# The first stage of a decoder block: where the x blocks are scaled, which engine makes the rotary angles, and the order of the first matmuls

## The chip, the cores and the metric

The kernel runs on one core of a Trainium2 chip. A core has five engines with a queue of instructions each, which run at the same time and wait for one another by semaphores: TensorE (PE in the profile; its weight loads are listed as PEld), VectorE (DVE), ScalarE (ACT), GpSimd (POOL) and SyncE (SP), which here only starts DMA transfers. SBUF is the on-chip memory of 128 partitions, PSUM the eight banks into which TensorE accumulates. The metric is the device time of one execution in microseconds (us), the median of several runs. A profile is one such execution with every instruction's start and end.

## The reference, cut to what matters

One layer of a decoder block on 1024 tokens of width 1024, in float32. What the change touches is the way from the input `x` to the first projection:

```python
ang = positions[..., None] * inv_freq                 # 8 frequencies
cos, sin = cos(ang), sin(ang)                         # rotate the queries and keys
cond = silu(c)
mod = cond @ w_ada + b_ada                            # six rows of 1024
sh_a, sc_a, gt_a, sh_m, sc_m, gt_m = split(mod, 6)
h = rms_norm(x, g_attn_pre) * (1 + sc_a) + sh_a
proj = h @ w_in                                       # 1024 x 2304
...                                                   # two mixers of attention, output projection, MLP
```

`rms_norm` divides each token's row by the root of its mean square and multiplies by a gain.

## The kernel before

**Products in two parts.** TensorE multiplies in a float32 form of fewer bits. So each operand is split: the high part is the value cast to that form, the low part is the value minus the high part. A product is then three matmuls: high x high, low x high, high x low. `hw[:, k, 0]` and `hw[:, k, 1]` are the high and the low part of h, row block k (128 of the 1024 features, all 1024 tokens); `w_hl[i]` holds both parts of a piece of `w_in`.

**The first stage.** `x` comes in as eight blocks of 128 tokens (`load_x`), 512 KB each, then `w_ada` in 16 pieces (`load_ada`, two for each row block k) and `w_in` in pieces (`load_w`), all in SP's queue. For each x block, `x_block(tb)` does:

1. ACT squares the block and sums each row (L652); DVE makes mean plus epsilon of it (`rsqrt_mean`, L477); POOL raises that to the power -1/2 (L480), which gives `rstd`, one number for each token.
2. The block is scaled by it and transposed on TensorE into a PSUM bank in two halves (g = 0, 1). There are two ways. In the first, DVE multiplies the block by `rstd` (L665) and TensorE transposes (L678). In the second (`wide_`), POOL builds a diagonal matrix of `rstd` (`dg`, L661) and TensorE multiplies the block by it (L676), which scales and transposes at once. Blocks 1, 3, 5, 6 and 7 go the second way.
3. ACT or DVE copies each half from PSUM to `xnT` (L686).

`mod_chunk(k)` then makes row block k of h: two reductions on DVE of `w_ada` against the broadcast `cond_b` (`gemv`, L697) give this row block's gain `g_a` and shift `s_a`; ACT applies them and writes the high part (`hi`, L710; for k = 0 in two halves of 512 tokens, L729) and the full value (`full`, L713; for the last k on DVE, L719); DVE subtracts (`lo`, L722). With even k a piece of `w_in` is split, in two halves: the cast on ACT (L557) and the subtraction on DVE (L560).

**The angles.** Position times frequency has to be brought into -pi to pi. This is a chain of 18 small instructions on 64 partitions x 128 elements on DVE (L635 to L641): one product, twice a rounding of two steps, 8 and 4 updates `ang = ang - part * kq`, and a clamp. The sine step `f_sin` on ACT (L746 to L750) loads another function table, makes the sines and cosines, and loads the first table again. Its result goes to DRAM and comes back, spread out, as the tables `cs_t` (L758, L759, L774), which the rotation of queries and keys reads (L826, L831).

**The first unit.** `first_unit` lists the matmuls of the first eight PSUM accumulators (four column blocks c, two halves of tokens) row block by row block, as triples (k, part, accumulator): part 0 is both products with the high part of h (L959, L961), part 1 the one with its low part (L963), and for k = 0 parts 2 and 3 are part 0 taken apart. `AHEAD = 6` row blocks are done for all accumulators before the rest is finished accumulator by accumulator.

**What sets the order.** No instruction is placed by hand. A planner (`Sched`) holds every step with its engine, an estimated duration, its dependences, the buffers it takes and gives, and a priority. It runs a clock for each engine, takes the step that can start first (the priority only breaks ties), and appends its instructions to the queue of that engine. So estimates decide the order in each queue; on the chip the queues then run in that order, and each instruction waits for its real operands. A dependence given to the planner alone (`ready`, `first_hi`, `behind`) thus moves a step in the order without adding a wait for data. `sc.dma`, `LAND` and the bytes per microsecond in `load` are its picture of the DMA.

The value reductions of `mod_chunk(0)` depend, in the planner, on the last block's scaling step, those of chunk 1 on the last eviction but one, and the others on the last four. The sine step depends on the angles and on `full` of chunk 1.

## Time and profile before

| | |
|---|---|
| median of 3 runs | 1112.44 us (1112.32 to 1112.46) |
| profiled execution | 1112.75 us, span of its instructions 1110.9 us |
| TensorE busy | 1091.5 us of the span |
| VectorE busy | 841.4 us |
| ScalarE busy | 648.1 us |
| GpSimd busy | 177.3 us |
| TensorE clock granted | 0.998 of full speed |

Times in the rows of the profile are counted from the start of the span. A row of the order of instructions reads: start, length, engine, line, operation, output <- inputs, shapes, count; in brackets how long the engine had been idle, and what ended that. A group of instructions reads: line, engine, operation, shapes, count | busy us, mean ns | idle us before them. A releaser is inferred from semaphores, and spans on GpSimd are rough. Idle time of an engine that isn't the bottleneck costs nothing by itself.

### The profile page before, as it was taken

What the parts mean: (1) busy time and instruction counts of PE and PEld (TensorE: products, weight loads), DVE (VectorE), ACT (ScalarE), POOL (GpSimd) and SP (SyncE); (2) the same over time, 40 slices, a digit from 0 to 9 for tenths busy, and PEclk for the clock granted to TensorE, in tenths of its full rate; (3) what the DMA queues carried; (4) which work ended last, traced back from release to release, by engine and by line L of the source; (5) the groups of instructions that cost most, each with busy time, mean ns of one, the idle gap of its engine ahead of it and who ended that gap; (6) DMA issues with size and microseconds to landing.
All of it is one profiled execution on the core that took longest, in us unless ns stands there. A gap on an engine that the chain in (4) does not pass through costs nothing.

```text
span 1110.9 us, 15895 instructions
## 1 busy us (share of the span) xinstructions
PE 1091.5 (98%) x5538; PEld 920.9 (83%) x5538; DVE 841.4 (76%) x1480; ACT 648.1 (58%) x1151; POOL 177.3 (16%) x225
## 2 busy tenths in 40 slices
PE   8999999999999999999999999999999999999997
PEld 7888888888988878888888888888888888888885
DVE  8975877888778876789698653898644996537997
ACT  7726666888866766687574234743145632247544
POOL 3004244564622321110000000000000000000003
PEclk9999999999999999999999999999999999999999
DMA  9866767677637526545851378511578013583006
GB/s 362 292 209 211 191 180 230 197 221 224 170 117 211 154 65 227 193 162 226 334 188 39 114 255 332 179 58 44 195 266 313 25 57 114 189 318 137 1 1 152
DMA packets 97432, 198.65 MB, mean 179 GB/s; under 512 B 8328, under 2 KB 31432, under 8 KB 97352
## 3 DMA queue, kind: packets, MB, share of 16 engines
q1 hardware_dynamic: 96632, 195.43, 52.2%
q0 software_dynamic: 576, 2.10, 1.1%
q8 instruction: 44, 0.72, 0.3%
q14 instruction: 36, 0.29, 0.1%
q10 hardware_dynamic: 144, 0.11, 0.0%
HBM read 155.46 MB, written 42.14 MB: 178 GB/s over the span
## 4 chain that ended last, share of the span: by engine, by line
PE 82%; DVE 8%; ACT 3%; DMA 2%; issue 2%; POOL 1%; SPq 0%; POOLq 0%; DVEq 0%; ACTq 0%
PE mlp_ps L2135 18%; PE mlp_ps L2136 18%; PE mlp_ps L2134 18%; PE s_ps L1245 2%; PE y_ps L1678 2%; PE y_ps L1680 2%; PE y_ps L1679 2%; PE pj L959 2%; PE pj L963 2%; PE pj L961 2%; PE o_ps L1379 1%; PE acc L959 1%; PE acc L961 1%; PE acc L963 1%; PE pt_ps L1349 1%
## 5 line engine op out<-in xcount | busy, mean ns | idle before, releaser
L2134 PE MATMUL mlp_ps<-hw 128*128 128x512 f32 x896 | 349.9, 391 | 0.0
L2135 PE MATMUL mlp_ps<-hw 128*128 128x512 f32 x896 | 349.0, 389 | 0.6 <-DVE hw L1899 0.6
L2136 PE MATMUL mlp_ps<-hw 128*128 128x512 f32 x896 | 348.9, 389 | 0.0
L2135 PEld LDWEIGHTS mlp_ps<-hw 128*128 128x128 f32 x896 | 168.3, 188 | 36.1 <-DVE hw L1899 1.0
L2134 PEld LDWEIGHTS mlp_ps<-hw 128*128 128x128 f32 x896 | 168.3, 188 | 35.2 <-issue 0.5
L2136 PEld LDWEIGHTS mlp_ps<-hw 128*128 128x128 f32 x896 | 168.3, 188 | 34.8
L1902 DVE TENSOR_TENSOR hw<-w,hw 128x1024 fp32r<-128x1024 f32 x94 | 111.8, 1223 | 106.7 <-ACT hw L1895 106.5
L1895 ACT CAST hw<-w 128x1024 fp32r<-128x1024 f32 x94 | 95.0, 1047 | 136.8 <-PE mlp_ps L2136 98.7
L2240 POOL TENSOR_TENSOR st<-st,nhalf 128x1 f32<-128x1 f32 x8 | 7.4, 926 | 596.6 <-DVE st L2237 596.5
L1895 ACT CAST hw<-u 128x1024 fp32r<-128x1024 f32 x48 | 48.7, 1052 | 64.6 <-PE mlp_ps L2136 64.6
L1367 DVE TENSOR_TENSOR ph<-pt_ps,ph 128x512 fp32r<-128x512 f32 (+1 forms) x110 | 68.9, 645 | 15.8 <-ACT ph L1363 14.9
L1363 ACT CAST ph<-pt_ps 128x512 fp32r<-128x512 f32 (+1 forms) x110 | 58.8, 555 | 21.7 <-PE pt_ps L1352 17.5
L1275 POOL TENSOR_SCALAR p_sb<-p_sb,den 128x128 f32<-128x128 f32 (+3 forms) x64 | 52.2, 818 | 118.7 <-DVE den L1273 102.5
L1137 POOL TENSOR_TENSOR ada_acc<-ada_acc,wa_st 128x512 f32<-128x512 f32 x42 | 55.8, 1329 | 95.8 <-ACT wa_st L1130 69.7
L1902 DVE TENSOR_TENSOR hw<-u,hw 128x1024 fp32r<-128x1024 f32 x48 | 57.1, 1223 | 16.7 <-ACT hw L1895 16.7
L959 PE MATMUL pj<-hw,w_hl 128*128 128x512 f32 x160 | 68.6, 429 | 0.0
L2192 DVE TENSOR_TENSOR yacc<-yacc,mlp_ps 128x512 f32<-128x512 f32 x96 | 62.6, 688 | 7.1 <-PE mlp_ps L2136 6.9
L963 PE MATMUL pj<-hw,w_hl 128*128 128x512 f32 x160 | 63.2, 395 | 0.0
L961 PE MATMUL pj<-hw,w_hl 128*128 128x512 f32 x160 | 63.0, 394 | 0.0
L1270 ACT ACTIVATE p_sb<-p_sb,mn 128x128 f32<-128x128 f32 (+3 forms) x64 | 49.7, 776 | 21.9 <-DVE mn L1263 20.5
L1678 PE MATMUL y_ps<-hw,oh 128*128 128x512 f32 x120 | 48.6, 405 | 0.9 <-DVE mn L1263 0.9
L1245 PE MATMUL s_ps<-kt,qt 128*128 128x512 f32 (+2 forms) x192 | 48.8, 352 | 0.3 <-DVE mn L1263 0.2
(218 smaller groups left out, 2097.5 us busy)
## 6 DMA issues: line engine op xcount, KB each, us to landing
hw<-s_dram SPq DMA_DIRECT2D x84, 512.0 KB, 4.4
wa_st<-in_w_ada SPq DMA_DIRECT2D x32, 512.0 KB, 5.3
w<-in_w_up SPq DMA_DIRECT2D x32, 512.0 KB, 5.0
w<-in_w_down SPq DMA_DIRECT2D x32, 512.0 KB, 8.9
s_dram<-hw SPq DMA_DIRECT2D x28, 512.0 KB, 4.9
qk_dram<-hl SPq DMA_DIRECT2D x52, 256.0 KB, 3.9
kt<-qk_dram SPq DMA_DIRECT2D x40, 256.0 KB, 6.1
w_st<-in_w_in SPq DMA_DIRECT2D x18, 512.0 KB, 4.6
```

What stands on the lines that cost most here:

```text
L959: T.matmul(ps, wt[:, 0, c0:c0 + P], hw[:, k, 0, t], start=(k == 0), stop=False)
L961: T.matmul(ps, wt[:, 1, c0:c0 + P], hw[:, k, 0, t], start=False, stop=False)
L963: T.matmul(ps, wt[:, 0, c0:c0 + P], hw[:, k, 1, t], start=False, stop=(k == KC - 1))
L1245: T.matmul(s[:, :cw], q_t[u, h, qb // 4][:, qb % 4 * P:qb % 4 * P + P], k_t[u, h, m][:, hl, :cw], start=(hl == 0), stop=(hl == 1))
L1367: V.tensor_tensor(b["ph"][:, 1, :w], b["pt"][:, :w], b["ph"][:, 0, :w].bitcast(F32), ALU.subtract)
L1678: T.matmul(ps[:], oh, wh, start=(k == 4 * i), stop=False)
L1895: A.copy(out[j][0], flat(src[j]))
L1902: V.tensor_tensor(out[j][1], flat(src[j]), out[j][0].bitcast(F32), ALU.subtract)
L2134: T.matmul(ps[m][:], sh, mh, start=starts and k == 0, stop=False, **kw)
L2135: T.matmul(ps[m][:], sh, ml_, start=False, stop=False, **kw)
L2136: T.matmul(ps[m][:], sl, mh, start=False, stop=k == 3, **kw)
L2192: e = op("DVE", t_dv(512), lambda: V.tensor_tensor(y(), y(), ps[m][:], ALU.add), [e, ml.e_y[tb, n]], gives=gives, prio=1)
```

## The change

All of it is in the first stage, and in the planner's picture of it.

- **x blocks.** Only blocks 3 and 5 keep the diagonal. The others are scaled on DVE; the last one in two halves of 512 features, of which the first half's transposes need only the first. The last power therefore goes straight to DVE. Evictions of blocks 0 to 2 are set to DVE, of blocks 4 to 7 to ACT; both evictions of the last block come, in the order, behind the first half of h's row block 0.
- **Angles.** They move to POOL, as 30 instructions: an update becomes a product and an addition. In POOL's queue they stand behind the last block's power. The sine step depends on `full` of chunk 4 instead of chunk 1.
- **Chunks.** All reductions depend, in the planner, on the last block's scaling only, and chunk 0 comes first among ties. `full` of chunk 0 comes behind `hi` of chunk 1.
- **Matmul order.** Row block 0's high products are taken half of the tokens by half, and the low products of row block k come behind the high products of row block k + 1.
- **The broadcast conditioning vector** is copied from PSUM by DVE instead of ACT.
- **The planner's DMA** gets another start, rate and landing time for the first 44 us.

```diff
-LAND = 1.6
+LAND, LAND_FIRST = 1.6, 1.05
...
-            end = self.dma + LAND
+            end = self.dma + (LAND if self.dma > 44 else LAND_FIRST)
...
-        return load(emit, nbytes, [before], takes=[(r, 1) for r in rings], prio=pri(), after=issued)
-
-    sc.dma = 0.5
+        return load(emit, nbytes * 345 / 412, [before], takes=[(r, 1) for r in rings], prio=pri(), after=issued)
+
+    sc.dma = 2.8
...
-            A.copy(cond_b[:, 512 * i:512 * i + 512], cond_ps[i][:])
-    e_cb = op("ACT", 2 * t_ps(512), f_cb, [e], gives=[(r_t, 2)], prio=0)
+            V.tensor_copy(cond_b[:, 512 * i:512 * i + 512], cond_ps[i][:])
+    e_cb = op("DVE", 2 * t_dv(512), f_cb, [e], gives=[(r_t, 2)], prio=3)
...
+    EARLY = 0
+    ON_DVE, ON_ACT = range(0, 6), range(8, 16)
+    WIDE = (3, 5)
...
+    red = p0.tile([64, P], F32, name="red")
+
+    def ts(o, i, c0, c1, f0, f1):
+        return lambda: G.tensor_scalar(o[:], i[:], c0, c1, f0, f1)
+    steps = [ts(ang, posf, inv_f[0:64], 1.0, ALU.mult, ALU.mult)]
...
+        steps += [ts(kq, ang, inv, ROUND, ALU.mult, ALU.add), ts(kq, kq, -ROUND, 0.0, ALU.add, ALU.add)]
         for part in parts:
-            steps += [lambda part=part: V.scalar_tensor_tensor(ang[:], kq[:], -part, ang[:], ALU.mult, ALU.add)]
...
+            steps += [ts(red, kq, -part, 1.0, ALU.mult, ALU.mult),
+                      lambda: G.tensor_tensor(ang[:], ang[:], red[:], ALU.add)]
+    steps += [ts(ang, ang, 3.1415925, -3.1415925, ALU.min, ALU.max)]
+    dg_last = Later()
     e = e_pos
-    for f in steps:
-        e = op("DVE", 0.22, f, [e, e_c], prio=1)
+    for i, f in enumerate(steps):
+        e = op("POOL", 0.45, f, [e, e_c] + [dg_last] * (i >= EARLY), prio=8)
...
-        wide_ = tb % 2 or tb == TB - 2
+        wide_ = tb in WIDE
...
-        else:
+        elif tb < TB - 1:
             e = op("DVE", t_d2(D) + AP_DV,
                    lambda: V.tensor_scalar(x_t[tb][:], x_t[tb][:], rstd[:, tb:tb + 1], None, ALU.mult), [e], prio=2)
+        else:
+            for i in range(2):
+                def f_sc(c=slice(512 * i, 512 * i + 512)):
+                    V.tensor_scalar(x_t[tb][:, c], x_t[tb][:, c], rstd[:, tb:tb + 1], None, ALU.mult)
+                e = es[i] = op("DVE", 0.42, f_sc, [e], prio=-1)
         e_scaled[0] = e
+        if tb == TB - 1:
+            dg_last.ev = e
...
-            e_xn.append(op(("ACT", "DVE"), (t_ps(512), t_dv(512)), (ev(A.copy), ev(V.tensor_copy)), [d] + [first_hi] * (tb == TB - 1 and g),
-                           gives=[(r_b, 1)], prio=2))
+            on = slice(1, 2) if 2 * tb + g in ON_DVE else slice(0, 1) if 2 * tb + g in ON_ACT else slice(0, 2)
+            e_xn.append(op(("ACT", "DVE")[on], (t_ps(512), t_dv(512))[on], (ev(A.copy), ev(V.tensor_copy))[on],
+                           [d] + [first_hi] * (tb == TB - 1), gives=[(r_b, 1)], prio=2))
...
-        ready = [e_scaled[0]] if k < 1 else e_xn[14:15] if k < 2 else e_xn[-4:]
+        ready = [e_scaled[0]]
...
-                gives=[(r_wa, 1)], prio=2)
+                gives=[(r_wa, 1)], prio=-1 if k < 1 else 2)
...
-            e = e_full[k] = op("ACT", t_sb(S) + 2 * AP_COST, full, e_hh[k], prio=0)
+            e = e_full[k] = op("ACT", t_sb(S) + 2 * AP_COST, full, e_hh[k] + [next_hi] * (not k), prio=0)
...
-    e_sin = op("ACT", 3.4, f_sin, [e_ang, e_full[1]], prio=0)
+    e_sin = op("ACT", 3.4, f_sin, [e_ang, e_full[4]], prio=0)
...
-        order = [(0, part, (c, half)) for part in (2, 3) for half in range(2) for c in (1, 0, 3, 2)]
-        order += [(k, part, a) for k in range(AHEAD) for part in range(not k, 2) for a in every]
+        order = [(0, part, (c, half)) for half in range(2) for part in (2, 3) for c in (1, 0, 3, 2)]
+        for k in range(1, AHEAD):
+            order += [(k - part, part, a) for part in range(2) for a in every]
+        order += [(AHEAD - 1, 1, a) for a in every]
```

More of the change, by code (lines that the diff above doesn't have):

```diff
@@ L633, in hybrid_block @@
     cs = p0.tile([64, 3, P], F32, name="cs")
-    steps = [lambda: V.tensor_scalar(ang[:], posf[:], inv_f[0:64], None, ALU.mult)]
+    red = p0.tile([64, P], F32, name="red")
+    def ts(o, i, c0, c1, f0, f1):
+        return lambda: G.tensor_scalar(o[:], i[:], c0, c1, f0, f1)
+    steps = [ts(ang, posf, inv_f[0:64], 1.0, ALU.mult, ALU.mult)]
     for inv, parts in ((1.0 / (TWO_PI * 4096), COARSE), (1.0 / TWO_PI, FINE)):
-        steps += [lambda inv=inv: V.tensor_scalar(kq[:], ang[:], inv, ROUND, ALU.mult, ALU.add),
-                  lambda: V.tensor_scalar(kq[:], kq[:], -ROUND, None, ALU.add)]
+        steps += [ts(kq, ang, inv, ROUND, ALU.mult, ALU.add), ts(kq, kq, -ROUND, 0.0, ALU.add, ALU.add)]
         for part in parts:
-            steps += [lambda part=part: V.scalar_tensor_tensor(ang[:], kq[:], -part, ang[:], ALU.mult, ALU.add)]
-    steps += [lambda: V.tensor_scalar(ang[:], ang[:], 3.1415925, -3.1415925, ALU.min, ALU.max)]
+            steps += [ts(red, kq, -part, 1.0, ALU.mult, ALU.mult),
+                      lambda: G.tensor_tensor(ang[:], ang[:], red[:], ALU.add)]
+    steps += [ts(ang, ang, 3.1415925, -3.1415925, ALU.min, ALU.max)]
+    dg_last = Later()
     e = e_pos
-    for f in steps:
-        e = op("DVE", 0.22, f, [e, e_c], prio=1)
+    for i, f in enumerate(steps):
+        e = op("POOL", 0.45, f, [e, e_c] + [dg_last] * (i >= EARLY), prio=8)
     e_ang = e
@@ L655, in x_block @@
         e = rsqrt_mean(rstd[:, tb:tb + 1], ssq[:, tb:tb + 1], D, 1, e, prio=0)
-        wide_ = tb % 2 or tb == TB - 2
+        wide_ = tb in WIDE
+        es = [None, None]
         box = {}
@@ L660, in f_dg @@
                 box["d"] = p0.tile([P, P], F32, name="dg", tag="dg", bufs=2)
-                G.tensor_scalar(box["d"][:], ident, rstd[:, tb:tb + 1], 1.0, ALU.mult, ALU.mult)
-            e = op("POOL", 0.39, f_dg, [e], takes=[(r_dg, 1)], prio=0)
-        else:
+                if tb < TB - 1:
+                    G.tensor_scalar(box["d"][:], ident, rstd[:, tb:tb + 1], 1.0, ALU.mult, ALU.mult)
+                else:
+                    V.tensor_scalar(box["d"][:], ident, rstd[:, tb:tb + 1], None, ALU.mult)
+            e = op("POOL" if tb < TB - 1 else "DVE", 0.39 if tb < TB - 1 else 0.25, f_dg, [e], takes=[(r_dg, 1)], prio=0)
+        elif tb < TB - 1:
             e = op("DVE", t_d2(D) + AP_DV,
                    lambda: V.tensor_scalar(x_t[tb][:], x_t[tb][:], rstd[:, tb:tb + 1], None, ALU.mult), [e], prio=2)
+        else:
+            for i in range(2):
+                def f_sc(c=slice(512 * i, 512 * i + 512)):
+                    V.tensor_scalar(x_t[tb][:, c], x_t[tb][:, c], rstd[:, tb:tb + 1], None, ALU.mult)
+                e = es[i] = op("DVE", 0.42, f_sc, [e], prio=-1)
         e_scaled[0] = e
+        if tb == TB - 1:
+            dg_last.ev = e
         r_x_ = r_stg if tb in IN_STG else r_wa
@@ L678, in tr @@
                         T.transpose(box[g][:, k], xk, ident)
-            d = pe_op("xt", 0.9 if wide_ else 0.46, tr, [e], takes=[(r_b, 1)],
+            d = pe_op("xt", 0.9 if wide_ else 0.46, tr, [es[g] or e], takes=[(r_b, 1)],
                       gives=([(r_x_, 1)] + [(r_dg, 1)] * wide_) if g else [])
@@ L724, in mod_chunk @@
             e_hh[k] = [op("ACT", t_sb(S) + 2 * AP_COST, hi, [e1, e2] + e_xn[k // 4::2], prio=0)] * 2
+            if k == 1:
+                next_hi.ev = e_hh[k][0]
         else:
```

3 lines of the change are left out of this document (2 added, 1 removed).

## The prediction

> **What bounds the kernel now.** I read the page's totals first, then a table of stages, then the chain of waits, then the order of instructions on each engine in the first 45 us.
>
> ```profile
> span 1110.9 us, 15895 instructions
> PE 1091.5 (98%) x5538; PEld 920.9 (83%) x5538; DVE 841.4 (76%) x1480; ACT 648.1 (58%) x1151; POOL 177.3 (16%) x225
> ```
>
> TensorE (PE) is busy for 98% of the span. The table of stages (stretch, its length, busy time of each engine with its count, granted clock, DMA share, GB/s) says where the rest is:
>
> ```profile
> 0.00:24.00 24.00, 19.26 (x135) 17.52 (x136) 19.73 (x68) 16.84 (x31) 10.86 (x17) 1.00 0.92 354
> 24.00:60.00 36.00, 36.00 (x160) 29.65 (x160) 32.51 (x44) 26.46 (x31) 0.00 (x0) 1.00 0.75 273
> 600.00:700.00 100.00, 100.00 (x440) 82.47 (x440) 53.75 (x58) 41.00 (x56) 0.00 (x0) 1.00 0.62 222
> ```
>
> From 24 us on PE hardly stops. So a microsecond by which PE's projection starts earlier is one off the end, if PE is then fed without a gap, and a new gap in the projection is one on the end. Before 24 us PE does only warm-up and transposes. The chain of waits there (start, length, what):
>
> ```profile
> 17.35 2.80 POOL rstd L480
> 20.23 0.89 POOL dg L661
> 21.16 1.17 PE pxt L676 x8
> 22.41 0.58 ACT xnT L686
> 23.00 0.72 ACT hw L729
> 23.76 2.11 PE acc L959 x8
> 33.15 1.81 PE acc L963 x8
> ```
>
> The projection starts at 23.76, and what it waits for is the last x block: the power on GpSimd (POOL), its diagonal, the scaling transposes, an eviction, and h's first half row. The power is far longer than its kind. In the order of instructions (start, length, engine, line):
>
> ```profile
> 8.42 0.55 POOL L480 TENSOR_TENSOR rstd<-rs_t,nhalf 128x1 f32<-128x1 f32 x1 [0.93 <-DVE rs_t L477]
> 16.74 0.37 POOL L661 TENSOR_SCALAR dg<-head,rstd 128x128 f32<-128x128 f32 x1
> 15.99 0.19 ACT L652 ACTIVATION_READ_ACCUMULATOR xnT<-x_sb 128x1 f32 x1
> 17.12 0.14 DVE L477 TENSOR_SCALAR rs_t<-ssq 128x1 f32<-128x1 f32 x1
> 17.18 1.33 DVE L697 CUSTOM_DVE_ANT_0 wa<-wa,cond_b,bb 128x1024 f32<-128x1024 f32 x1
> 17.35 2.79 POOL L480 TENSOR_TENSOR rstd<-rs_t,nhalf 128x1 f32<-128x1 f32 x1 [0.23 <-DVE rs_t L477]
> 18.45 1.28 DVE L697 CUSTOM_DVE_ANT_0 wa<-wa,cond_b,bb 128x1024 f32<-128x1024 f32 x1
> 20.23 0.88 POOL L661 TENSOR_SCALAR dg<-head,rstd 128x128 f32<-128x128 f32 x1
> 20.26 0.70 DVE L560 TENSOR_TENSOR w_hl<-w_st,w_hl 128x512 fp32r<-128x512 f32 x1 [0.52 <-ACT w_hl L557]
> ```
>
> The power takes 0.55 at 8.42 and 2.79 at 17.35. In between, VectorE (DVE) runs the two reductions of w_ada chunk 0 (L697) until 18.45 + 1.28 = 19.73, and the power ends 0.41 after that. The diagonal takes 0.37 alone and 0.88 beside a subtraction that ends at 20.96; it ends 0.15 later. So a POOL instruction that reads SBUF stands still while DVE runs one with two SBUF inputs. This observation carries the forecast, in both directions.
>
> **The change, part by part: the gain.** The last block loses its diagonal (0.88) and its slow power: the reductions of chunk 0 now come behind the block's scaling. Its transposes become plain ones. The statistics step (L477) starts at 17.12, though its square's sum is there at 16.18 (15.99 + 0.19): DVE's queue held two evictions and the angles' last step ahead of it. Both kinds leave DVE, so I start from 16.2. The prices of the rest:
>
> ```profile
> L665 DVE TENSOR_SCALAR x_sb<-x_sb,rstd 128x1024 f32<-128x1024 f32 x3 | 2.2, 745 | 0.2 <-POOL rstd L480 0.2
> L729 ACT ACTIVATE hw<-xnT,s_a,g_a 128x512 fp32r<-128x512 f32 x2 | 1.5, 809 | 0.0
> L619 ACT COPY cond_b<-cond_ps 128x512 f32<-128x512 f32 x2 | 1.1, 577 | 0.0
> L640 DVE SCALAR_TENSOR_TENSOR ang<-kq,ang 64x128 f32<-64x128 f32 x12 | 3.4, 285 | 0.1
> ```
>
> Statistics 0.15, power 0.55, two half scalings 0.8 (one whole is 0.745, each half pays its start again: estimate), two reductions 2.55, handovers 0.1: 16.2 + 4.15 = 20.35. Then h's first half row, 0.8, whose eviction (blocks 0 to 3) is long done: PE starts at 21.2 instead of 23.76, 2.55 earlier. The half scalings and the transposes of the last block lie beside the reductions; h's second half is needed 8 matmuls (1.8 us) later, and two evictions and the activation (about 1.9 us on ScalarE, ACT) take as long: 0 to 0.3 lost. Chunk 1 is the next bound. It must be done when 16 matmuls of row block 0 are, at 21.2 + 16 x 0.2265 = 24.8 (0.2265 is the pitch of the chain's matmuls, 1.81 for 8 at 33.15). DVE reaches it at 21.07, as its first row below shows for before, then 2 x 1.27 and ACT's 1.24: 24.9. I take **2.4 us** for the whole gain (2.55 less 0.15), with 1.4 and 2.6 as ends: the lower one if a half of w's split stands ahead of chunk 1 (0.7) and POOL slows DVE by 0.3.
>
> The conditioning copies (0.58 each) change from ACT to DVE and three more blocks are scaled on DVE (3 x 0.745) where three diagonals fall away; the 12 steps of 0.285 and six others leave DVE. All this lies before 16.2 us, where x comes in at the DMA's pace: +-0.3, in the ends. That h's low products come one row block later moves 8 matmuls; it removes none.
>
> **The change, part by part: the loss.** 30 angle steps (one, twice two, 12 updates that now need two instructions each, and the clamp: 18 with one input, 12 with two) go to POOL behind the last power. A 64 x 128 step on POOL isn't in the trace. Its nearest rows are the 0.37 above and the power's 0.55: about 0.42, so 30 steps alone take some 12.5 us, from 16.9 to 29.4. They won't be alone. From 21 to 45 us DVE did this (groups: count, busy us, mean ns), without a pause:
>
> ```profile
> L697 DVE CUSTOM_DVE_ANT_0 wa<-wa,cond_b,bb 128x1024 f32<-128x1024 f32 x11 | 14.2, 1314 | 0.1
> L722 DVE TENSOR_TENSOR hw<-xnT,hw 128x1024 fp32r<-128x1024 f32 x5 | 6.1, 1223 | 0.4 <-ACT xnT L713 0.4
> L560 DVE TENSOR_TENSOR w_hl<-w_st,w_hl 128x512 fp32r<-128x512 f32 x5 | 3.4, 688 | 0.0
> 30.00:40.00 10.00, 10.00 (x45) 8.19 (x45) 10.00 (x16) 9.94 (x15) 0.00 (x0) 1.00 1.01 398
> 21.09 1.35 DVE L697 CUSTOM_DVE_ANT_0 wa<-wa,cond_b,bb 128x1024 f32<-128x1024 f32 x1
> ```
>
> 21 instructions in 24 us, 1.14 each, all with two SBUF inputs. What such a neighbour does to POOL shows again later:
>
> ```profile
> 487.25 1.63 POOL L1725 TENSOR_TENSOR st<-rs_t,nhalf 128x1 f32<-128x1 f32 x1 [5.07 <-DVE rs_t L1723]
> 487.25 1.23 DVE L1902 TENSOR_TENSOR hw<-h,hw 128x1024 fp32r<-128x1024 f32 x1
> 488.39 1.22 DVE L2067 TENSOR_TENSOR sum_T<-w,sum_T 128x1024 f32<-128x1024 f32 x1
> 202.90 2.26 DVE L560 TENSOR_TENSOR w_hl<-w_st,w_hl 128x1024 fp32r<-128x1024 f32 x1
> ```
>
> At 487 the power gets in between two DVE instructions, at 17.35 it had to let two go by, and at 202.90 DVE waited for POOL. So POOL gets one step through for each DVE instruction at best (a step's first 0.2 us passes before it asks, and by then DVE has started the next), and one for two at worst. I take one for one, the nearer to most rows.
>
> [...]
>
> Who waits for the angles? The sine step on ACT, which now stands behind the full row of chunk 4, and behind it in ACT's queue h's chunks 5 to 7 (and the table writes on SP's queue, and what SP has behind those):
>
> ```profile
> 28.50 1.28 ACT L746 ACT_TABLE_LOAD   x1
> 32.26 0.31 ACT L750 ACTIVATE ang<-kq 64x128 f32<-64x128 f32 x1
> 61.99 0.69 DVE L826 TENSOR_TENSOR hl<-acc,cs_t 64x512 f32<-64x512 f32 x1 [2.91 <-PE acc L963]
> 40.21 1.24 ACT L713 ACTIVATE xnT<-xnT,s_a,g_a 128x1024 f32<-128x1024 f32 x1
> 44.25 1.25 ACT L710 ACTIVATE hw<-xnT,s_a,g_a 128x1024 fp32r<-128x1024 f32 x1 [2.29 <-DVE s_a L697]
> 51.13 0.39 PE L959 MATMUL acc<-hw,w_hl 128*128 128x512 f32 x1
> ```
>
> The sine step takes 32.57 - 28.50 = 4.1 with its two table loads. Chunk 4's full row ran at 40.21; ACT no longer makes the sine detour before it, but DVE sets its pace, so ACT reaches the sine step at about 41. By then DVE has ended 5 such instructions before 21 and (41 - 21) / 1.14 = 17 after: 22 angle steps done, 8 left. DVE still has work of its own that doesn't need ACT (chunks 5, 6, half of 7), so 8 x 1.0 more: angles at 49, sine at 53.1, h's chunk 5 at 54.3. PE wants chunk 5 (first used at 51.13 now) 2.4 earlier, and 8 matmuls (1.8) earlier again since a low product has moved behind it: 46.9. PE waits **7.4 us**. Ends: 3.9 us if a step comes through every 0.95 us (16.9 + 30 x 0.95 = 45.4, and 5.3 for sine and chunk 5); 12 if POOL gets in once for two DVE instructions: DVE's own work, some 28 instructions, ends at 21 + 23 x 1.14 = 47 with 14 steps done, and 16 x 0.42 more make it 53.7.
>
> Once fed, PE isn't held again: chunks 6 and 7 each have 5.4 us of its matmuls ahead of them against ACT's 2.5. The rotation tables come 11 us later than the sine (writes and loads on SP's queue: estimate), at 64, and the first accumulator, which the rotation takes up at 61.99 now, would then be done near 67.
>
> **The sum.** The profiled execution took 1112.75 us (span 1110.9 and 1.85 around it), 0.3 over the median of the runs. 1112.75 - 2.4 + 7.4 = 1117.75; as a median **1117.4 us**.
>
> **Rivals.** (1) **The angles keep up.** If a step comes through every (41.6 - 16.9) / 30 = 0.82 us or faster, they are done when ACT gets to the sine or just after, chunk 5 is ready at 41.6 + 5.3 = 46.9, and the gain stands: 1112.4 - 2.4 = 1110.0. For it: 12.5 us of work have 24.7 us of room, and DVE may pause for landings. Against it: the 17.35 and 20.23 rows, and DVE's 10.00 of 10. This is the case of the other sign, and 0.82 us a step is where it begins. (2) **Gain and stall cancel.** With 0.85 to 0.95 us a step PE waits 0.8 to 3.9 us: 1110.9 to 1113.9, say 1112.4. (3) **The start doesn't move as far**, since the last x block lands as before and ACT's evictions stand ahead of its squares: gain 1.4, so 1111.0 in rival 1 and 1118.4 in my case.
>
> **How the numbers follow.** Late angles 0.47 (its own range 1113.9 to 1122), keeping up 0.38, cancelling 0.15. Faster and slower count from 0.2% (2.2 us), about what a measurement can tell. Faster: 0.34, nearly all of rival 1 (the rest, 0.04, with the small gain of 3, is within). Slower: 0.48, the late angles and a little of the cancelling case. Within: 0.18. Rival 3 is a smaller gain inside either case, with 0.15 of each. Range 1109.7 to 1121.5, from nearly the full gain of rival 1 to just under POOL's worst rate, as cases of both signs hold most of the chance.
>
> **What would show it.** Right: the projection's first matmul near 21.2; the last power at 0.55; angle steps on POOL of 1 us and more from 21 us on, the last near 49; ACT idle ahead of the sine's table load, released by POOL; PE idle ahead of row block 5, near 47. Wrong: angle steps mostly under 0.8 us, or the sine load right behind chunk 4's full row; then rival 1 holds. The start of the projection at 22.5 or later would break the gain.

## The result, and the profile after

The changed kernel takes 1118.86 us (median of 6 runs, 1117.86 to 1120.33) against 1112.45 us before (6 runs, 1111.78 to 1112.69): a ratio of 1.0059, with a 95% interval of 1.0049 to 1.0069. It is slower by 6.4 us. The forecast was 1117.4, in a range of 1109.7 to 1121.5. The profiled execution of the changed kernel took 1117.86 us, 5.1 more than the profiled one of before.

The page's totals of the changed kernel say that TensorE (PE) does the same work in a longer span, and GpSimd (POOL) 25 us more of its own (177.3 before):

```profile
span 1116.1 us, 15864 instructions
PE 1091.7 (98%) x5514; PEld 918.8 (82%) x5514; DVE 841.8 (75%) x1463; ACT 649.4 (58%) x1154; POOL 202.3 (18%) x252
```

The table of stages of the changed kernel (stretch, length, busy time of PE, its weight loads, DVE, ACT and POOL with their counts, granted clock, DMA share, GB/s) shows where. Before, PE was busy for 36.00 of the 36 us of the first row:

```profile
24.00:60.00 36.00, 30.18 (x123) 23.67 (x122) 31.44 (x42) 24.60 (x28) 24.14 (x23) 0.95 0.61 227
600.00:700.00 100.00, 100.00 (x440) 82.42 (x440) 53.69 (x55) 40.98 (x55) 0.00 (x0) 1.00 0.56 202
```

In the 36 us of the first projection PE now lacks 5.8 us, VectorE (DVE) and ScalarE (ACT) are less busy too, and the mean granted clock is 0.95 instead of 1.00. The long MLP stage, in the second row, is as before. So the loss lies between 24 and 60 us. In the order of instructions on POOL there (start, length, engine, line; L641 and L647 are the angle steps), a selection:

```profile
16.15 0.99 POOL L480 TENSOR_TENSOR rstd<-rs_t,nhalf 128x1 f32<-128x1 f32 x1 [0.33 <-DVE rs_t L477]
17.13 0.36 POOL L641 TENSOR_SCALAR ang<-posf,head 64x128 f32<-64x128 f32 x1
...
21.08 0.62 POOL L641 TENSOR_SCALAR red<-kq 64x128 f32<-64x128 f32 x1
21.78 1.34 POOL L647 TENSOR_TENSOR ang<-ang,red 64x128 f32<-64x128 f32 x1
...
48.87 1.15 POOL L641 TENSOR_SCALAR ang<-ang 64x128 f32<-64x128 f32 x1
```

The first step takes 0.36 and the second 0.34, the later ones 0.62 to 1.49, and the last ends at 48.87 + 1.15 = 50.02: 30 steps in 32.9 us, 1.10 each. What stands behind them on ACT, and then on PE (L769 to L773 is the sine step, L731 h's high part, L982 and L984 the first unit's matmuls; the bracket is the idle time before, and what ended it), in the same view of the changed kernel:

```profile
40.84 1.24 ACT L734 ACTIVATE xnT<-xnT,s_a,g_a 128x1024 f32<-128x1024 f32 x1
42.61 1.28 ACT L769 ACT_TABLE_LOAD   x1
50.05 0.31 ACT L769 ACTIVATE cs<-ang 64x128 f32<-64x128 f32 x1 [6.15 <-POOL ang L641]
51.20 1.28 ACT L773 ACT_TABLE_LOAD   x1
52.72 1.23 ACT L731 ACTIVATE hw<-xnT,s_a,g_a 128x1024 fp32r<-128x1024 f32 x1
...
21.59 1.20 PE L982 MATMUL acc<-hw,w_hl 128*128 128x512 f32 x4 [1.44 <-ACT hw L752]
26.39 0.50 PE L984 MATMUL acc<-hw,w_hl 128*128 128x512 f32 x1 [0.35 <-DVE w_hl L560]
53.99 0.80 PE L982 MATMUL acc<-hw,w_hl 128*128 128x512 f32 x1 [4.95 <-ACT hw L731]
```

PE starts the projection at 21.59 instead of 23.76, 2.17 us earlier. At 42.61 ACT comes to the sine, loads the table, and stands for 6.15 us until POOL has the angles. Chunk 5 of h, behind the sine in ACT's queue, is ready at 53.95; PE had run out of other matmuls and starts row block 5 at 53.99, after an idle time of 4.95. Then comes something that the forecast doesn't have. The same stretch of the changed kernel in windows of 2 us (stretch, length, PE's busy time and count, granted clock, DMA share, GB/s):

```profile
52.00:54.00 2.00, 0.01 (x1) 0.87 0.21 49
54.00:56.00 2.00, 2.00 (x5) 0.50 0.22 50
56.00:58.00 2.00, 2.00 (x9) 0.77 0.90 286
58.00:60.00 2.00, 2.00 (x10) 1.00 0.93 256
```

After the gap the granted clock is 0.50 for some 3 us. The first eight matmuls take 3.29 us (53.99 to 57.28) where eight take 1.81: 1.5 us more are lost. The rotation takes up the first accumulator at 68.14 instead of 61.99, and the MLP starts at 494.49 instead of 489.25.

### The profile page after: what moved, and what is told of

Read it like the earlier page. It is cut to its first block, busy times and chain, and to the rows that moved or that the text cites. A ratio compares the mean times of both kernels' runs of the same rounds, so it can differ in the third digit from the quotient of the medians.

```text
span 1116.1 us, 15864 instructions
## 1 busy us (share of the span) xinstructions
PE 1091.7 (98%) x5514; PEld 918.8 (82%) x5514; DVE 841.8 (75%) x1463; ACT 649.4 (58%) x1154; POOL 202.3 (18%) x252
## 4 chain that ended last, share of the span: by engine, by line
PE 85%; DVE 7%; POOL 3%; ACT 2%; issue 2%; DMA 0%; POOLq 0%; DVEq 0%; SPq 0%; ACTq 0%
PE mlp_ps L2160 17%; PE mlp_ps L2159 17%; PE mlp_ps L2161 17%; PE pj L982 3%; PE pj L986 3%; PE pj L984 3%; PE s_ps L1270 3%; PE y_ps L1703 2%; PE y_ps L1705 2%; PE y_ps L1704 2%; PE s_ps L1324 2%; PE o_ps L1404 2%; POOL ang L647 1%; PE o_ps L1415 1%; PE pt_ps L1374 1%
## 5 line engine op out<-in xcount | busy, mean ns | idle before, releaser
L1300 POOL TENSOR_SCALAR p_sb<-p_sb,den 128x128 f32<-128x128 f32 (+3 forms) x64 | 50.8, 797 | 104.8 <-DVE den L1298 83.7
L982 PE MATMUL pj<-hw,w_hl 128*128 128x512 f32 x160 | 68.1, 426 | 0.0
L984 PE MATMUL pj<-hw,w_hl 128*128 128x512 f32 x160 | 63.0, 393 | 0.0
L1270 PE MATMUL s_ps<-kt,qt 128*128 128x512 f32 (+2 forms) x192 | 48.9, 353 | 0.9 <-DMA qt<-qk_dram 0.4
```

The lines of the kernel that those rows point to most:

```text
L982: T.matmul(ps, wt[:, 0, c0:c0 + P], hw[:, k, 0, t], start=(k == 0), stop=False)
L984: T.matmul(ps, wt[:, 1, c0:c0 + P], hw[:, k, 0, t], start=False, stop=False)
L1270: T.matmul(s[:, :cw], q_t[u, h, qb // 4][:, qb % 4 * P:qb % 4 * P + P], k_t[u, h, m][:, hl, :cw], start=(hl == 0), stop=(hl == 1))
```

## The experiments

Late angles (theory L, the prediction's) blame the queue: the sine waits on ACT, and chunk 5 behind it. The rivals at first were P, that GpSimd's angle steps slow DVE beside them wherever the sine stands, and O, that the loss comes from the new matmul order or the evictions. All runs together, in us; "start" is PE's first projection matmul, "rotation" the first instruction of DVE that takes up an accumulator (L826 before, L849 after the change), "MLP" PE's first MLP matmul, all from the profiled execution:

| kernel | median (lowest to highest) | ratio to before, 95% interval | start | rotation | MLP | profiled |
|---|---|---|---|---|---|---|
| before | 1112.45 (1111.78 to 1112.69) | | 23.76 | 61.99 | 489.25 | 1112.75 |
| changed | 1118.86 (1117.86 to 1120.33) | 1.0059, 1.0049 to 1.0069 | 21.59 | 68.14 | 494.49 | 1117.86 |
| 1 coarse updates out | 1112.06 (1111.56 to 1113.04) | 0.9997, 0.9987 to 1.0006 | 21.89 | 61.02 | 488.29 | 1111.64 |
| 2 sine one chunk later | 1113.97 (1112.62 to 1115.25) | 1.0013, 1.0003 to 1.0022 | 21.41 | 61.82 | 490.53 | 1113.89 |
| 3 angles from the start | 1116.19 (1114.53 to 1117.10) | 1.0032, 1.0020 to 1.0044 | 22.88 | 63.00 | 491.21 | 1115.70 |
| 4 angles on VectorE | 1117.17 (1116.81 to 1119.13) | 1.0047, 1.0031 to 1.0064 | 22.82 | 64.73 | 493.36 | 1116.81 |
| 5 angles alone | 1117.27 (1116.88 to 1119.25) | 1.0045, 1.0030 to 1.0060 | 22.22 | 67.41 | 493.93 | 1117.38 |
| 6 matmul order of before | 1117.83 (1115.09 to 1118.95) | 1.0043, 1.0028 to 1.0058 | 21.95 | 66.24 | 495.56 | 1118.95 |
| 7 gap filled | 1118.60 (1117.50 to 1119.22) | 1.0053, 1.0038 to 1.0068 | 22.39 | 67.60 | 494.10 | 1117.50 |
| 8 planner's price | 1116.25 (1115.00 to 1117.33) | 1.0032, 1.0020 to 1.0045 | 21.35 | 69.32 | 492.65 | 1116.09 |
| 9 angles shared | 1113.65 (1113.35 to 1115.03) | 1.0014, 1.0005 to 1.0023 | 21.23 | 64.44 | 490.19 | 1113.59 |
| 10 shared, in one piece | 1111.84 (1111.03 to 1114.37) | 0.9997, 0.9988 to 1.0006 | 21.46 | 61.42 | 488.38 | 1111.78 |

The kernel before ran beside each group of runs, with medians of 1112.28 (runs 1 to 4), 1112.47 (5 to 8), 1112.31 (9) and 1112.83 (10); the ratios are to those. From the MLP's start on all of them take 623.4 us, to 0.1 (run 3 1.1 more), so what differs has come in by then. The start itself varies by some 0.6 us either way among the runs whose first 20 us are alike (the changed kernel and 1, 2, 7, 8, 9 and 10).

### 1: the coarse updates left out

```diff
-                      lambda: G.tensor_tensor(ang[:], ang[:], red[:], ALU.add)]
+                      lambda: G.tensor_tensor(ang[:], ang[:], red[:], ALU.add)] if parts is FINE else [lambda: None] * 2
```

> The changed kernel with its 16 coarse update instructions of the angles left out (the angles are then not reduced; nothing else is left out, and every queue keeps its order). Theory L (late angles block the scalar engine's queue, and so row block 5 of h): 14 steps of about 1.05 us from 17.1 end near 32, the sine step runs at 42.6 without a wait, h's row block 5 is ready near 48 where TensorE wants it at 48.9; TensorE's gap of 5.1 us and its slow 3 us after it go: 6.6 us less than the changed kernel's 1118.9, so 1112.3, down to 1111.3 if TensorE's two small waits in row blocks 1 and 3 go too. [...] Rival O (the new matmul order or the evictions made the loss): 1118 to 1119.

Measured: 1112.06. In the order of instructions of this kernel, POOL's last angle step, ACT's table load and the first rotation:

```profile
30.20 1.15 POOL L641 TENSOR_SCALAR ang<-ang 64x128 f32<-64x128 f32 x1
41.94 1.28 ACT L769 ACT_TABLE_LOAD   x1
61.02 0.69 DVE L849 TENSOR_TENSOR hl<-acc,cs_t 64x512 f32<-64x512 f32 x1 [2.90 <-PE acc L986]
```

With 14 steps instead of 30 the angles are there at 31.35, 10 us before ACT wants them, PE has no gap, and 6.8 us of the changed kernel's 1118.86 are gone. So the 16 steps cost 6.8 us; this run alone doesn't tell their lateness from what they do to DVE beside them (run 2 does). What is left of the change is worth 0.2 us by the medians (1112.06 against 1112.28), no difference that can be measured (the interval reaches from 1.4 us faster to 0.7 slower), although PE starts 1.87 us earlier than before. 0.6 of that goes ahead of row block 1, where PE waits for the split of w on DVE (L560: PE's matmuls at 25.68 and 26.53 lie 0.85 apart instead of 0.2265), another 0.3 in smaller pieces; at the rotation 0.97 is left.

### 2: the sine one chunk later

```diff
-    e_sin = op("ACT", 3.4, f_sin, [e_ang, e_full[4]], prio=0)
+    e_sin = op("ACT", 3.4, f_sin, [e_ang, e_full[5]], prio=0)
```

> The changed kernel with the sine step behind the full row of chunk 5 instead of chunk 4; all angle steps stay where they are, TensorE's queue is the same. Theory L: row block 5 is ready near 45, the angles still end near 50, the sine at 52.8, row block 6 near 54 where TensorE wants it at 56; the tables land near 61.3, in time for the first accumulator near 61.5. So 1112.3 (1118.9 - 6.6), with all of VectorE's and GpSimd's delays still there. Rival P: the steps are unchanged, so 1118 to 1119. Rival O: the same, 1118 to 1119.

Measured: 1113.97, where L said 1112.3. The sine on ACT, and PE much later, in the order of instructions of this kernel:

```profile
49.85 0.31 ACT L769 ACTIVATE cs<-ang 64x128 f32<-64x128 f32 x1 [2.45 <-POOL ang L641]
...
372.49 0.50 PE L1404 MATMUL o_ps<-ph,v_hl 128*128 128x256 f32 x2 [2.01 <-DVE ot L1444]
```

and the clock behind that last row, in this kernel's windows of 2 us:

```profile
372.00:374.00 2.00, 1.51 (x6) 0.74 0.54 144
374.00:376.00 2.00, 2.00 (x10) 0.50 0.79 228
```

In the first stage L is right: chunk 5 stands ahead of the sine, PE has no gap there, although the angles come no earlier (49.81) and ACT waits for them as well, and the rotation starts at 61.82. One moved instruction takes 4.9 us off the changed kernel, with all 30 steps in place; the 1118 to 1119 of P and O falls. P isn't nothing, though: from PE's start to the rotation run 2 needs 40.41 us (61.82 - 21.41) and run 1, with 16 steps fewer, 39.13, so up to 1.3 of run 1's 6.8 us are what GpSimd does to DVE. Of the 1.7 us that are missing 1.5 lie between the rotation and the MLP (428.7 us, 427.3 before), in the attention stage: PE waits 2.01 us at 372 and then runs at half clock again. With the change the planner also writes another order for that stage. The kernel before has no such wait; the changed one, whose order on PE is the same as in run 2, has it with 1.42 us (377.58) and without a fall of the clock. What makes it 2.01 here is not settled. Four of the ten executions take 1112.62 to 1113.06, near L's number, the others up to 1115.25.

### 3 and 4: the angles elsewhere

Run 3 lets the steps begin as soon as the positions are there; run 4 puts them back on VectorE in their form of before and leaves the rest of the change.

```diff
-    EARLY = 0
+    EARLY = 30
```

```diff
-        e = op("POOL", 0.45, f, [e, e_c] + [dg_last] * (i >= EARLY), prio=8)
+        e = op("DVE", 0.22, f, [e, e_c], prio=1)
```

> The changed kernel with the angle steps free to start as soon as the positions are there, so that they stand between the powers of the x blocks in GpSimd's queue instead of behind the last one. Theory L: while VectorE mostly evicts PSUM, a step takes 0.35 to 0.5 us; a power waits up to 0.5 us for the step ahead of it, so the projection starts 0.3 to 0.8 us later than 21.6; the angles end near 30, the sine no longer waits: 1110.5 to 1112.5. Rival P: the same number of steps beside the same VectorE work, 1116 or more. Rival O: 1118 to 1119.

> The changed kernel with the angles on VectorE as before (18 instructions), all else changed, the sine still behind chunk 4. Theory L: the gain of the change without its loss. 18 x 0.28 = 5 us go back into VectorE's queue ahead of 18 us; where they fit between x blocks the projection starts near 22 and the time is 1110.5, where they don't it starts near 23.5 and the time is 1112. Rival O: 1116 or more, as the angles aren't the cause.

Measured: 1116.19 and 1117.17. L missed both; by the numbers alone P's "1116 or more" is met in run 3 and O's in run 4. The traces show another reason than theirs. The gap ahead of row block 5 is gone in both, as L says; but the angles now stand in the way of the x blocks. Run 3, PE and POOL in the order of instructions:

```profile
35.84 1.15 POOL L641 TENSOR_SCALAR ang<-ang 64x128 f32<-64x128 f32 x1
...
22.88 1.19 PE L982 MATMUL acc<-hw,w_hl 128*128 128x512 f32 x4 [1.04 <-ACT hw L752]
28.67 0.50 PE L984 MATMUL acc<-hw,w_hl 128*128 128x512 f32 x1 [0.89 <-DVE w_hl L560]
```

Run 4, DVE and PE in the same view:

```profile
21.88 0.74 DVE L673 TENSOR_SCALAR x_sb<-x_sb,rstd 128x1024 f32<-128x1024 f32 x1
...
14.65 0.66 PE L693 MATMUL pxt<-head,x_sb 128*128 128x128 f32 x4 [2.50 <-DVE rs_t L477]
22.82 1.18 PE L978 MATMUL acc<-hw,w_hl 128*128 128x512 f32 x4 [0.55 <-ACT hw L748]
24.07 1.94 PE L693 MATMUL pxt<-head,x_sb 128*128 128x128 f32 x16
27.52 1.20 PE L978 MATMUL acc<-hw,w_hl 128*128 128x512 f32 x4 [0.81 <-ACT hw L748]
```

In run 3 the steps stand between the powers, the last power starts at 17.34 instead of 16.15, PE starts at 22.88 and then waits 0.89 for w's split. Up to 17 us its steps take 0.29 to 0.65; from 19.68 on, beside DVE's reductions and subtractions, 0.62 to 1.54. In run 4 one whole block is scaled only at 21.88, behind both reductions of chunk 0; PE starts at 22.82, but 16 transposes then stand between its first matmuls, and h's second half comes at 27.52. Both also have the wait near 374 us (1.95 and 1.74), with a granted clock of 0.50 in a window of 2 us behind it. In the profiled executions run 3 is 1.0 us later than before at the rotation, another 0.95 at the MLP and another 1.0 at the end, the last for no reason that a run shows; run 4 is 2.7 later at the rotation and another 1.4 at the MLP. So with the angles among the x blocks, on either engine, PE's early start is lost in part, and the waits behind it take more than what is left.

### 5: the angles alone

The kernel before, with the steps on GpSimd and the sine behind chunk 4's full row, as in the change; everything else as before.

```diff
-    steps = [lambda: V.tensor_scalar(ang[:], posf[:], inv_f[0:64], None, ALU.mult)]
+    steps = [ts(ang, posf, inv_f[0:64], 1.0, ALU.mult, ALU.mult)]
...
-        e = op("DVE", 0.22, f, [e, e_c], prio=1)
+        e = op("POOL", 0.45, f, [e, e_c] + [dg_last], prio=8)
...
-    e_sin = op("ACT", 3.4, f_sin, [e_ang, e_full[1]], prio=0)
+    e_sin = op("ACT", 3.4, f_sin, [e_ang, e_full[4]], prio=0)
```

> The kernel before with one part of the change: the 30 angle steps on GpSimd behind the last block's work and the sine step behind chunk 4's full row; scaling, conditioning copies and matmul order as before. Theory L (late angles hold ScalarE's queue): the steps start near 21 us, after the last diagonal, and take 1.10 us each as in the changed kernel, so they end at 54; the sine needs 2.7 more, chunk 5 another 1.2: ready at 58. TensorE wants it near 51.5, waits 6.5 us and then runs at half clock for about 3 us (1.5 lost): 1112.4 + 8 to 8.5 = 1120 to 1121, worse than the whole change. Rival O (the loss comes from the new matmul order or the scaling, not from the angles): 1114 or less.

Measured: 1117.27; L's 1120 to 1121 was 3 us too much, rival O falls. In the order of instructions of this kernel:

```profile
19.51 0.37 POOL L638 TENSOR_SCALAR ang<-posf,head 64x128 f32<-64x128 f32 x1
49.45 0.29 POOL L638 TENSOR_SCALAR ang<-ang 64x128 f32<-64x128 f32 x1
...
22.22 2.12 PE L966 MATMUL acc<-hw,w_hl 128*128 128x512 f32 x8 [0.55 <-ACT hw L736]
54.23 0.80 PE L966 MATMUL acc<-hw,w_hl 128*128 128x512 f32 x1 [4.09 <-ACT hw L717]
```

This one part gives 4.8 of the 6.4 us, with the same gap ahead of row block 5. What the expectation didn't have: without the angles on DVE the kernel before starts at 22.22 already. That is 1.54 of the 2.17 us by which the whole change moves the start. Its statistics step comes at 16.68 instead of 17.12, and its power gets in after one reduction, where before it had to let two go by:

```profile
16.91 1.58 POOL L480 TENSOR_TENSOR rstd<-rs_t,nhalf 128x1 f32<-128x1 f32 x1 [0.29 <-DVE rs_t L477]
```

That is 1.58 instead of 2.79, and most of the 1.54. The halves, the reductions' places and the evictions together add some 0.6, no more than the start scatters by. The steps began at 19.51, earlier than I had them, took 30.2 us, 1.01 each, and the gap was 4.1 instead of 6.5.

### 6: the matmul order of before

```diff
-        order = [(0, part, (c, half)) for half in range(2) for part in (2, 3) for c in (1, 0, 3, 2)]
-        for k in range(1, AHEAD):
-            order += [(k - part, part, a) for part in range(2) for a in every]
-        order += [(AHEAD - 1, 1, a) for a in every]
+        order = [(0, part, (c, half)) for part in (2, 3) for half in range(2) for c in (1, 0, 3, 2)]
+        order += [(k, part, a) for k in range(AHEAD) for part in range(not k, 2) for a in every]
```

> The changed kernel with the matmul order of before in the first unit (each chunk's low-part products directly behind its high-part products, not one row block later). Theory L: chunk 5 is ready at 54 us whatever TensorE does before, and 8 matmuls (1.8 us) that now stand behind that point stand ahead of it again, inside the gap: the gap falls from 5.1 to 3.3 us, the first accumulator comes 1.8 us earlier (66.3 instead of 68.1), 1116.0 to 1117.0. A stall for a low part before chunk 5 (up to 3 us) would be inside the gap too and cost nothing. Rival O (the new order saves more than 1.8 us of waits earlier): 1118.9 or more.

Measured: 1117.83, first rotation at 66.24 (L: 66.3). The rotation came out as expected by luck, for it got there by another way. PE in the order of instructions of this kernel, and then its windows:

```profile
23.62 1.74 PE L982 MATMUL acc<-hw,w_hl 128*128 128x512 f32 x4 [0.48 <-ACT hw L752]
30.06 3.13 PE L986 MATMUL acc<-hw,w_hl 128*128 128x512 f32 x8 [1.82 <-DVE hw L743]
```

```profile
24.00:26.00 2.00, 2.00 (x6) 0.51 1.03 414
32.00:34.00 2.00, 2.00 (x6) 0.50 1.02 408
```

With the old order PE waits early: 0.48 us for h's second half, soon after the 1.44 ahead of its start, and 1.82 us for a low part of h (L743), both times with half clock after it. So it is late by itself, and there is no gap left ahead of row block 5. The new matmul order (row block 0 half by half, the low parts one row block later) spares these waits. But chunk 5 comes at 54.3 all the same, and all that PE saves ahead of it ends in the gap. The whole isn't told apart from the changed kernel: at 1115.09 to 1118.95 the four runs scatter too far, and this profiled one has the attention wait with 2.04 us on top.

### 7: the gap filled

```diff
+            def fillers():
+                for i in range(22):
+                    T.matmul(accs[every[i % 8]][:], zt[:], hw[:, 4, 0, 0:512], start=False, stop=False)
+            if k == 5 and part == 0 and a == every[0]:
+                dense(0.0, fillers, [])
```

> The changed kernel with 22 more matmuls (128 x 512, a weight tile of zeros, so they add nothing to the accumulators) ahead of row block 5 on TensorE: 22 x 0.2265 = 4.98 us of work where TensorE waited 5.1 us. Nothing else is changed. Theory C (the half clock after the gap comes from TensorE standing idle): the clock stays at 1.00, the 1.5 us behind the gap fall away, first accumulator at 66.6 instead of 68.1, 1116.4 to 1117.4. Rival (the clock falls for another reason, such as all engines starting at once behind the wait): the clock falls as before, 1117.9 to 1119.

Measured: 1118.60, profiled 1117.50. The 22 matmuls in the order of instructions, and PE's windows around them:

```profile
49.69 5.31 PE L1006 MATMUL acc<-hw,zt 128*128 128x512 f32 x22
```

```profile
48.00:52.00 4.00, 4.00 (x19) 1.00 0.00 0
52.00:56.00 4.00, 4.00 (x18) 1.00 0.17 40
56.00:60.00 4.00, 4.00 (x19) 1.00 0.79 238
```

The clock stays at 1.00 throughout, and from PE's start to the first rotation it takes 45.21 us instead of 46.55: 1.34 less, with 22 matmuls more. So the half clock comes from PE standing idle (theory C), not from the restart. On the whole time this doesn't show; 1118.60 lies in the rival's range, and only the trace speaks for C. The start lay 0.8 us later in this execution (22.39), and single runs scatter by more than the 1.3 us.

### 8: the planner told the price

```diff
-        e = op("POOL", 0.45, f, [e, e_c] + [dg_last] * (i >= EARLY), prio=8)
+        e = op("POOL", 1.10, f, [e, e_c] + [dg_last] * (i >= EARLY), prio=8)
```

> The changed kernel with one number of the planner altered: an angle step on GpSimd is entered at 1.10 us, as the trace of the changed kernel shows it, instead of 0.45. The planner then puts the sine step behind h's chunk 7 on ScalarE, at about 53 us, and the steps themselves stay where they are. Theory L: no gap ahead of row block 5, first accumulator complete near 61.5; the rotation tables come 11 us behind the sine, at about 65, so the first rotation waits some 3 us on its tables, of which TensorE feels part: 1112 to 1115. Rival (the loss is the slower VectorE beside GpSimd, not the queue order): 1116 or more.

Measured: 1116.25, over L's 1112 to 1115 and inside the rival's "1116 or more". The trace shows another reason than the rival's. In the order of instructions of this kernel:

```profile
69.32 0.69 DVE L849 TENSOR_TENSOR hl<-acc,cs_t 64x512 f32<-64x512 f32 x1
86.40 0.39 PE L1059 MATMUL pj<-w_hl,hw 128*128 128x256 f32 x1 [2.78 <-DVE hl L820]
```

There is no gap ahead of row block 5. But the planner moved the sine from 42.61 to 54.66, and the rotation starts at 69.32, 8 us later than in run 1: the tables' loads are issued only from 62.85 to 68.7 and land 4.3 us later (the median), where I had 65 for the tables. In DVE's queue a split of w, which ends at 69.29, stands ahead of it as well; which of the two held it isn't told apart. PE feels it at 86.40, with 2.78 us and half clock behind it (0.89, 0.50 and 0.76 in the windows of 2 us from 86 to 92). With 1.5 to 1.7 us for that clock (1.5 as in the changed kernel, 1.7 by these windows: (0.11 + 0.50 + 0.24) x 2) these are about the 4.4 us by which it is later than run 1 at the MLP, so the slower VectorE isn't needed to explain the time; it isn't excluded as a small part of it. The planner's low price explains why the sine was put ahead of chunk 5; the right price alone only moves the wait to the other end.

### 9 and 10: the angles shared

Product and coarse half stay on GpSimd behind the last power, the fine half and the clamp go to VectorE as one-instruction updates. In run 9 the planner places them one by one, in run 10 they stand in one piece.

```diff
+    steps += [("DVE", lambda: V.tensor_scalar(kq[:], ang[:], 1.0 / TWO_PI, ROUND, ALU.mult, ALU.add)),
+              ("DVE", lambda: V.tensor_scalar(kq[:], kq[:], -ROUND, None, ALU.add))]
+    for part in FINE:
+        steps += [("DVE", lambda part=part: V.scalar_tensor_tensor(ang[:], kq[:], -part, ang[:], ALU.mult, ALU.add))]
+    steps += [("DVE", lambda: V.tensor_scalar(ang[:], ang[:], 3.1415925, -3.1415925, ALU.min, ALU.max))]
...
-        e = op("POOL", 0.45, f, [e, e_c] + [dg_last] * (i >= EARLY), prio=8)
+        e = op(eng, 1.10 if eng == "POOL" else 0.3, f, [e, e_c] + [dg_last] * (i >= EARLY), prio=8 if eng == "POOL" else 0)
```

and, in run 10, the last lines instead:

```diff
+    fine = [f for eng, f in steps if eng == "DVE"]
+    for i, f in enumerate([f for eng, f in steps if eng == "POOL"]):
+        e = op("POOL", 1.10, f, [e, e_c] + [dg_last] * (i >= EARLY), prio=8)
+    e = op("DVE", 1.7, lambda: [f() for f in fine], [e], prio=-2)
```

> The changed kernel with the angles shared out: the first 17 steps (the product and the coarse half of the reduction) stay on GpSimd behind the last power, the other 8 (the fine half, as one-instruction updates, and the clamp) go back to VectorE, where the planner places them; it is told 1.10 us for a step on GpSimd. Theory L: GpSimd's steps end near 17 + 17 x 1.1 = 36 us, VectorE's 8 take some 2.3 us more and end before 46, the planner puts the sine behind chunk 6's full row, chunk 5 is ready near 45 to 48, before TensorE wants it at 48.9: no gap ahead of row block 5, clock 1.00 up to 100 us, first accumulator near 61.5 to 62; the 2.2 us won at the start are spent on small waits as in the run without the coarse updates: 1111.5 to 1113.5, no difference from before. Rival (VectorE is the bound of these 25 us, so 2.3 us more on it come out at the end): 1114 to 1115, with TensorE waiting for chunk 6 or 7.

> The run with the shared angles (first 17 steps on GpSimd, last 8 on VectorE), but the 8 steps on VectorE stand in one piece instead of between its other instructions, so that they end near 45 instead of 51 us and the planner puts the sine behind chunk 5's full row (about 46 to 49 us) instead of chunk 6's (52 to 56). Theory L: the tables land before 61, the first rotation has no wait on them, h's chunk 7 no longer stands behind the sine, and the waits of 0.8 and 0.5 us for it go: first accumulator near 61.5 to 62.5, 1111.5 to 1113. Rival (VectorE's 2.3 us more come out at the end wherever they stand): as the run with the shared angles, 1113.5 to 1114.5.

(The counts in both are off: 19 steps stay on GpSimd, 7 go to VectorE.) Measured: 1113.65 and 1111.84. Run 9 lies between L's 1111.5 to 1113.5 and the rival's 1114; PE and DVE in its order of instructions:

```profile
57.40 0.50 PE L986 MATMUL acc<-hw,w_hl 128*128 128x512 f32 x1 [0.78 <-ACT hw L735]
64.44 0.69 DVE L853 TENSOR_TENSOR hl<-acc,cs_t 64x512 f32<-64x512 f32 x1 [0.68 <-DMA cs_t<-cs_dram]
```

and the same of run 10:

```profile
43.62 1.24 DVE L651 SCALAR_TENSOR_TENSOR ang<-kq,ang 64x128 f32<-64x128 f32 x4
47.07 0.31 ACT L775 ACTIVATE cs<-ang 64x128 f32<-64x128 f32 x1
61.42 0.69 DVE L855 TENSOR_TENSOR hl<-acc,cs_t 64x512 f32<-64x512 f32 x1 [2.62 <-PE acc L992]
```

In run 9 the pieces end at 50.8, the sine stands ahead of chunk 7 (0.78 us on PE) and the tables are 0.68 late. In run 10 the same instructions end at 45.1, the sine runs from 45.78 without a wait on the angles, and both waits are gone. That takes all of the changed kernel's loss away; 2 us more on VectorE at 43 us cost nothing that shows, and the rival falls by the trace. By the times it falls less clearly: of the eleven executions six take 1111.03 to 1111.84 and five 1113.05 to 1114.37, and what parts them no run shows. Nor does it beat the kernel before: 1111.84 against 1112.83 measured beside it looks like a gain, but the ratio is given as 0.9997 with an interval that reaches to both sides of 1.

## Why the prediction was right, and where not

**The likeliest case came true.** Late angles were forecast at 1117.4; the changed kernel takes 1118.86, and runs 1, 2 and 5 show that it is this mechanism in the main: shorten the angles and 6.8 us go; take chunk 5 out from behind the sine, with the angles as late as before, and 4.9 go; do the angles alone and 4.8 come.

**The angles' rate: right.** One step for each DVE instruction was forecast to end at 49; the steps took 1.10 us each and ended at 50.02. The count agrees too: from 18.01 on 28 steps stand beside 28 two-input instructions of DVE, from 18.13 to 51.1. That a step's first 0.2 us pass before it "asks" was an estimate (0.37 less the 0.15 of the 20.23 row); no run shows that part of a step by itself. The two groups of steps in the changed kernel between 17 and 51 us (count, busy time, mean ns, idle before):

```profile
L647 POOL TENSOR_TENSOR ang<-ang,red 64x128 f32<-64x128 f32 x12 | 15.2, 1270 | 1.0
L641 POOL TENSOR_SCALAR red<-kq 64x128 f32<-64x128 f32 x12 | 10.0, 830 | 1.0
```

Two-input steps cost 1.27, one-input ones 0.83, where the first, before DVE's reductions, took 0.36. The price of the other side was not in the sum (up to 1.3 us, run 2 against run 1): a reduction of w_ada on DVE that meets a two-input step on POOL takes 1.47, as this row of the changed kernel's order of instructions shows (beside POOL's 21.78 row above), instead of 1.27 to 1.33:

```profile
22.73 1.47 DVE L718 CUSTOM_DVE_ANT_0 wa<-wa,cond_b,bb 128x1024 f32<-128x1024 f32 x1
```

**The wait ahead of row block 5: right in kind, 5.1 us instead of 7.4.** Two terms were off. The sine needed 2.7 us behind the angles, not 4.1, since its first table load (42.61) doesn't wait for the angles and lay inside the wait. And PE came to row block 5 at 48.9, not 46.9: 0.4 from the start, 0.6 ahead of row block 1, 0.5 ahead of row block 3 (37.85), the rest in smaller pieces. The angles came 1.0 later than forecast, which takes back most of the sine's 1.4; so chunk 5 itself was ready at 53.95, forecast 54.3.

**A term that was missing: the clock.** The gap of 4.95 us cost 1.5 us more: the granted clock was 0.50 for the first 3 us or so behind it, and eight matmuls took 3.29 us instead of 1.81. With it the loss, from PE's start to the first rotation, is 46.55 - 38.23 = 8.3 us (5.1 of wait, 1.5 of clock, 1.7 of small waits ahead of row block 5), and 8.3 - 2.2 = 6.1 is what the rotation shows (68.14 against 61.99).

**The gain: the step that failed.** "I take 2.4 us for the whole gain" was right at its own place: PE starts 2.17 us earlier. It was wrong as a term of the sum, because it goes on to the end only if PE is then fed without a gap. Run 1 has the early start (1.87) and no late angles, and is worth 0.2 us by the medians, 1.1 by the profiled executions. I named the reason as a lower bound (a half of w's split in the way, 0.7: measured 0.6), and took 1.4 for the worst, which was still too much. DVE is busy for all of the 27.8 us from 17.2 to 45 in the changed kernel, so an earlier PE runs into a DVE that isn't earlier. So rival 1 would have been mispriced as well: with the angles in time it isn't 1110.0 but about 1112, as runs 1 and 10 show. Loss and gain were both taken too large (7.4 and 2.4 for 6.8 and 0.2), and the errors went against each other. That 7.4 lies so near 6.8 is luck: the wait was taken 2.3 us too long, while the clock's 1.5 and the small waits ahead of row block 5 were not in the sum. And a loss that was taken 0.6 too large hides a part of a gain that was taken 2.2 too large.

**Small slips in the working.** With a step every 0.95 us the wait comes to 45.4 + 5.3 - 46.9 = 3.8, not 3.9. The row read as "DVE reaches chunk 1 at 21.07" says 21.09 (it was 21.47 in the changed kernel). And DVE of before did pause in the stretch from 21 to 45 us, 0.81 us up to 23.25 and 0.35 up to 26.10. None of them moves the forecast by more than 0.1 or so.

**Why the start moved** was only partly as told. The last power did not take 0.55 but 0.99 (16.15): another block's scaling on DVE, which has one SBUF input only, ran beside it until 16.73, and the power ended 0.41 after that, the very delay that the prediction read behind the reductions:

```profile
15.99 0.74 DVE L677 TENSOR_SCALAR x_sb<-x_sb,rstd 128x1024 f32<-128x1024 f32 x1
```

So "DVE with two SBUF inputs" was too narrow: a scaling with one held the power too, 0.99 instead of 0.55. And 1.54 us of the earlier start come with taking the angles off DVE (run 5), which the forecast counted only as queue ahead of the statistics step; there the power got its place one reduction earlier.

**"Once fed, PE isn't held again"** held: the tables landed in time (their loads were issued from 55.5 to 60.0 and took 3.5 us to land, the median, ahead of the rotation at 68.14), and behind row block 5 PE isn't held up to the rotation. From there to the MLP the changed kernel is 0.9 us faster than before (426.35 against 427.26), for which no run gives the cause; with this the 6.1 become 5.2 at the MLP and 5.1 in the profiled times. The medians are 6.4 apart, and the difference between those two is within the scatter of the runs.

## What to carry to other kernels

An operation moved to an idle engine is priced by what its neighbours leave it, not by its time alone: here 0.36 became 1.10 beside a VectorE that was busy for all of the 33.8 us from 17.2 to 51, one step for each of its instructions, and the planner, which had 0.45, put the consumer ahead of work that TensorE needed. A queue in order makes a late input into a wait for everything behind it (here 6.15 us on ScalarE, and 4.95 on TensorE for the chunk behind the sine), so ask of such a consumer what stands behind it, when its input comes, and when its own result is due: the sine cost nothing at 45.8 us with the angles there, and something both at 42.6 without them and at 52 and 54.7, where its tables came late. A start that is moved forward is worth only what the next engine can follow (run 1's 1.87 us came to 0.2 by the medians); look at whether that engine has pauses before counting it to the end.
